# Fourteen of 24 branch gates of a hybrid decoder step as seven pairs of seven block products

## The chip, the cores and the metric

The kernel runs on one NeuronCore of a Trainium2 chip. Five engines work side by side on one on-chip memory (SBUF): PE (TensorE, matrix products into PSUM), DVE (VectorE), ACT (ScalarE), POOL (GpSimd) and SP (SyncE, which here issues every DMA, in one queue and in order). The metric is the device time of one execution in microseconds (us), as the median of several runs.

## The reference: what is computed

One layer of a decoder for a prompt of 1024 tokens and a sample group of 8 x 4 tokens, 1056 columns in all, model width 1024. What concerns the change is the mixer block:

```python
h = _rmsnorm(x, norm_g)
p = h @ w_in
cuts = np.cumsum(IN_WIDTHS)[:-1].tolist()
q, k, v, g, su, sv, xq, gt = jnp.split(p, cuts, axis=-1)
...
g_ret, g_sg, g_x = jnp.split(jax.nn.sigmoid(gt + b_gate), N_BRANCH, axis=-1)
merged = g_ret * (o_ret @ w_br_ret) + g_sg * (o_sg @ w_br_sg) + g_x * (o_x @ w_br_x)
return x + merged @ w_o, S_new, v_rows
```

`gt` holds three gates of 1024 channels each, so 3 x 8 tiles of 128 channels. A feed-forward block follows (2 x 2816 channels up, a causal convolution, a gated gelu, down), and a last norm.

## The kernel before

Activations lie transposed: a tile `[128 x 1056]` holds 128 channels (on partitions) of all columns, and 1024 channels are eight tiles. Every product is made from two rounded parts, high and low, of each operand: high x high, high x low, low x high, three matmuls in place of one. `split` (L285) makes the parts: ACT casts to the high one, then POOL (`ptt`, L114) or DVE (`vtt`, L111) subtracts to get the low one. `hops` are the parts of the eight input tiles without the norm's factor; `scaled` (L348) multiplies a product by that factor per column (`rst`) when it is taken out of PSUM, and the norm's gain sits in the weights.

Weights come from DRAM as slabs of `[128 x 1024]` in the order of the table SLABS (L43 ff.). `w_dma` (L132) loads one into `wr` (two buffers), `w_prep` (L140) makes `wh` on ACT (L150) and `wl` on POOL (three buffers each); a slab's load can start only when the subtraction two slabs back has freed its `wr`.

`fm` (L227) makes one tile of 128 output channels: per 128-channel step k three terms by three column chunks (384, 384, 288), so 72 matmuls of a gate over eight k, 36 of a half-slab product over four, into one of two PSUM buffers `mp`. After each k it calls `hook` (L189), where delayed work (`later`) and generators (`gens`, at `rate` steps a hook) put their instructions: cross-attention `xattn`, or `reload`, which reads a branch's output back from DRAM (`opr<-scr`) and splits it. Each engine executes its instructions in the order in which the program is written.

The stretch that matters, in order: eight gates `gb` (with the last heads of the cross-attention woven into them), gates `gc` 0 and 1 (with the reload of the spatial branch's operands `bops`), eight half-slab products `bs`; then in turn a gate `gc` m+2, half a slab of `bx`, and their sum on POOL; eight gates `ga` (the retention operand is reloaded by `rd`, `rs_`); eight products `br` with the merge; the output product `wo`; the feed-forward block. A gate tile `th` is taken from PSUM by DVE, gets its tanh on ACT and stays in SBUF until `gated` multiplies the branch product into it. `slot` (L90) hands out all such tiles from one pool of 40.

The up-projection of the feed-forward block is written another way already. Two output tiles make a pair. Their two slabs, each cut into two halves of the 1024 input channels, are four blocks a11, a12, a21, a22; the operand is cut by halves of the channels and of the columns (528) into four blocks too. The 2x2 product of such blocks takes seven block products instead of eight, with sums of weight blocks (s1 to s4, `f_sums`, `f_prep0` to `f_prep3`) and of operand blocks (B11, B21, B22, T1 to T4, split by `x_split`). `prod` makes one block product: four k, three terms, two chunks of 264 columns, 24 matmuls into a PSUM buffer `bp`; `put` takes it out on ACT, or on DVE with an addition.

Names in the rows: `ap` is a PSUM buffer of the attention (two of them), `xt`, `xmx`, `xrc`, `pt`, `ox`, `ys` its tiles, `ssq` and `c` tiles of the feed-forward block, `x2c` the residual.

Of the kernel before, what the change touches and what calls it, by code (L numbers as in the profile page):

```python
# [42 lines left out]
def slab_order():  # L43
# [8 lines left out]
    o += [("gc", 0), ("gc", 1)]  # L52
    o += [("bs", j) for j in range(4)]
    for m in range(8):
        if m < 6:
            o += [("gc", m + 2)]
        if m % 2 == 0:
            o += [("bx", m // 2)]
    o += [("ga", m) for m in range(8)]
# [19 lines left out]
def step_kernel(ctx: ExitStack, tc: tile.TileContext, xT, memT, wslab, cst, ident_d, rope, vec, sgc, sgm, sgs,  # L79
# [50 lines left out]
    raws, hil, wst = {}, {}, {"d": 0, "p": 0, "live": 0, "end": FAST0, "max": 3}  # L130
# [41 lines left out]
    gens = deque()  # L172
# [179 lines left out]
    with tc.manual_schedule():  # L352
# [780 lines left out]
        def gate(key, br, m):  # L1133
            ps = fm(key, hops)
            t = slot("th")
            scaled(t, ps)
            act(t, t, AF.Tanh, scale=0.5, bias=vecs[:, VBG + 8 * br + m:VBG + 8 * br + m + 1])
            return t

        def gated(t, ps):  # L1140
            for o, i in zip(seg(t), psv(ps)):
                stt(o, o, 1.0, i, ALU.add, ALU.mult)

        bops, cops, aops = [], [], []
        acc, thc = [], []
        for m in range(8):
            acc.append(gate(("gb", m), 1, m))
        bg = reload([8 + g for g in range(4)], bops)
        cg = reload([12 + g for g in range(4)], cops)
        drain()  # L1150
        rate[0] = 0.5
        gens.append(bg)
        thc.append(gate(("gc", 0), 2, 0))
        thc.append(gate(("gc", 1), 2, 1))
        drain()
        rate[0] = 0.0
        for m in range(8):
            ps = fm(("bs", m // 2), bops, kbase=4 * (m % 2), free=(m % 2 == 1))
            gated(acc[m], ps)
            if m in (1, 3, 5, 7):  # L1160
                next(cg)
        gens.append(cg)
        rate[0] = 1.0
        for m in range(8):
            if m < 6:
                thc.append(gate(("gc", m + 2), 2, m + 2))
            drain()
            ps = fm(("bx", m // 2), cops, kbase=4 * (m % 2), free=(m % 2 == 1))
            gated(thc[m], ps)
            ptt(acc[m], acc[m], thc[m], ALU.add)  # L1170

        raw = {}

# [8 lines left out]
        def late():
            for k in range(2, 8):
                rs_(k)
                rd(k + 3)
                yield

        tha = []
        rate[0] = 1.0
        for m in range(8):  # L1190
            if m == 3:
                rd(0)
                rd(1)
                rd(2)
            if m == 5:
                rs_(0)
                rd(3)
            if m == 6:
                rs_(1)
                rd(4)  # L1200
            if m == 7:
                gens.append(late())
            tha.append(gate(("ga", m), 0, m))
        drain()
        mops = [[], []]
        for m in range(8):
            ps = fm(("br", m), aops)
            gated(tha[m], ps)
            vtt(acc[m], acc[m], tha[m], ALU.add)

            for half in range(2):
                t = slot("mg", F32R)
                src = acc[m][:, half * HW:(half + 1) * HW]
                nc.scalar.copy(out=t[:, 0:HW], in_=src)
                ptt(t[:, HW:2 * HW], src, f(t)[:, 0:HW], ALU.subtract)
                mops[half].append(t)


        x2c = []
        for m in range(8):  # L1220
            x2c.append(slot("x2c"))
            dma(x2c[m], xT[m])
        ssq = slot("ssq")
        hsl = slot("hist")
        dma(hsl[:, 0:NHC], hist)
        hv_ = hsl[:, 0:NUP * 16].rearrange("p (m b j) -> p m b j", b=8, j=2)
        coll = slot("coll", shape=[P, NUP, 18])

        X = {}

        def hs(k, half):
            return x2c[k][:, half * HW:(half + 1) * HW]
# [17 lines left out]
        nrm = {}  # L1250

        def norm_sums(half):
            s3 = nrm["s3"] = slot("ns3", F32R)
            src = ssq[:, half * HW:(half + 1) * HW]
            nc.scalar.copy(out=s3[:, 0:HW], in_=src)
            vtt(s3[:, HW:2 * HW], src, f(s3[:, 0:HW]), ALU.subtract)

        def norm_root(half):
            s3, t = nrm["s3"], slot("nst")
            r = rst[:, half * HW:(half + 1) * HW]  # L1260
            for q in range(2):
                a = ap()[:, 0:QW]
                c = slice(q * QW, (q + 1) * QW)
                mm(a, ones, s3[:, q * QW:(q + 1) * QW], stop=False)
                mm(a, ones, s3[:, HW + q * QW:HW + (q + 1) * QW], start=False)
                rstd_sum(a, r[:, c], t[:, c])
            newton(r, t[:, 0:HW], t[:, HW:2 * HW])

        def h_scale(k, half):
            stt(hs(k, half), hs(k, half), vecs[:, VNF + k:VNF + k + 1], rst[:, half * HW:(half + 1) * HW], ALU.mult, ALU.mult)  # L1270

        def half_norm():

            low = lambda k: x_low(("B11", "B21")[k // 4], k % 4, hs(k, 0), vtt)
            norm_sums(0)
            yield
            norm_root(0)
            for k in range(8):
                h_scale(k, 0)
                x_split(("B11", "B21")[k // 4], k % 4, hs(k, 0), None)  # L1280
                if k:
                    low(k - 1)
                yield
            low(7)

# [44 lines left out]
        def f_prep3(j):  # L1330
# [660 lines left out]
```

## Time and profile before

| What | us |
|---|---|
| median of 3 runs | 1932.78 (1932.71 to 1933.3) |
| profiled execution, its time | 1929.98 |
| profiled execution, its span | 1928.2 |
| granted TensorE clock, mean | 0.994 of full speed |
| PE busy | 1870.1 |
| DVE, POOL, ACT busy | 1055.6, 913.3, 620.0 |

A timeline row gives start, length, engine, line, operation, result tile <- source tiles, size and type, how many (x4), and in brackets how long the engine was idle before and what released it. The rows of section 6 of the page name a DMA, how many, KB each, and the median us from its issue to its landing. The page's slices of the span, 48.2 us each, show where the edit lies, in slices 16 to 24 (690 to 1135 us):

```profile
PE   8999999999999999999999999999999999999997
...
DVE  7464636443464441111112257999999999744447
...
POOL 2343434232643425334264444477777778753404
PEclk9999999999999999999999999999999999999998
...
GB/s 197 44 45 99 37 113 45 113 66 155 56 136 86 110 36 154 34 55 45 89 89 45 182 139 100 34 73 84 78 82 75 77 90 98 260 144 89 76 1 91
```

### The profile page before, as it was taken

The numbers are of one execution on the slowest core, as the hardware profiler recorded it, in microseconds if no ns is written. First come the engines' busy times: TensorE is split into PE (matmuls) and PEld (weight loads), VectorE is DVE, ScalarE is ACT, GpSimd is POOL, SyncE is SP. The second block draws the span as 40 slices with busy tenths as digits, with TensorE's granted clock in tenths as the row PEclk, the third lists the DMA queues.
The fourth block names the chain that finished last, engine by engine and source line by source line (L and its number), as shares of the span: only waits on it lengthen the run. The fifth ranks groups of instructions, "written<-read, shape, count | busy, mean of one in ns | idle before, by whom it ended". The sixth has DMA issues, their size and how long they took to land.

```text
span 1928.2 us, 31394 instructions
## 1 busy us (share of the span) xinstructions
PE 1870.1 (97%) x13201; PEld 1844.8 (96%) x13201; DVE 1055.6 (55%) x1509; ACT 620.0 (32%) x966; POOL 913.3 (47%) x569
## 2 busy tenths in 40 slices
PE   8999999999999999999999999999999999999997
PEld 8999998999999999999999999899999999899996
DVE  7464636443464441111112257999999999744447
ACT  6322232422233432111231234534344344321204
POOL 2343434232643425334264444477777778753404
PEclk9999999999999999999999999999999999999998
DMA  5113131324132314111221443122222223742202
GB/s 197 44 45 99 37 113 45 113 66 155 56 136 86 110 36 154 34 55 45 89 89 45 182 139 100 34 73 84 78 82 75 77 90 98 260 144 89 76 1 91
DMA packets 51741, 174.51 MB, mean 91 GB/s; under 512 B 5712, under 2 KB 8944, under 8 KB 51600
## 3 DMA queue, kind: packets, MB, share of 16 engines
q1 hardware_dynamic: 51600, 172.50, 26.5%
q8 instruction: 104, 1.70, 0.4%
q14 instruction: 37, 0.30, 0.0%
HBM read 137.04 MB, written 35.43 MB: 89 GB/s over the span
## 4 chain that ended last, share of the span: by engine, by line
PE 80%; DVE 11%; ACT 4%; issue 3%; POOL 1%; DMA 0%; DVEq 0%; SPq 0%; ACTq 0%; POOLq 0%
PE mp L106 56%; PE bp L106 20%; PE ap L106 4%; DVE c L118 1%; DVE xl L112 1%; DVE x2c L118 1%; ACT sw L476 1%; ACT wh L150 0%; DVE ssf L112 0%; DVE fs L112 0%; DVE st L526 0%; DVE rt L118 0%; PE ap L576 0%; DVE x L112 0%; DVE th L112 0%
## 5 line engine op out<-in xcount | busy, mean ns | idle before, releaser
L115 POOL TENSOR_TENSOR wl<-wr,wh 128x1024 fp32r<-128x1024 f32 x114 | 297.1, 2610 | 474.8 <-ACT wh L150 410.6
L106 PE MATMUL mp<-hh,wh 128*128 128x384 f32 (+1 forms) x1152 | 261.3, 334 | 5.8 <-ACT hh L109 5.8
L106 PE MATMUL mp<-hl,wh 128*128 128x384 f32 (+1 forms) x1152 | 253.0, 327 | 0.0
L106 PE MATMUL mp<-hh,wl 128*128 128x384 f32 (+1 forms) x1152 | 250.1, 324 | 0.0
L106 PE MATMUL bp<-xh,wh 128*128 128x264 f32 (+2 forms) x1040 | 212.5, 285 | 4.5 <-DVE z L112 2.1
L106 PE MATMUL bp<-xh,wl 128*128 128x264 f32 (+2 forms) x1040 | 212.2, 286 | 0.1
L106 PE MATMUL bp<-xl,wh 128*128 128x264 f32 (+2 forms) x1040 | 211.5, 285 | 0.0
L106 PEld LDWEIGHTS mp<-hh,wh 128*128 128x128 f32 x1152 | 190.9, 190 | 8.1 <-ACT hh L109 5.8
L106 PEld LDWEIGHTS mp<-hh,wl 128*128 128x128 f32 x1152 | 193.4, 189 | 0.0
L106 PEld LDWEIGHTS mp<-hl,wh 128*128 128x128 f32 x1152 | 192.2, 189 | 1.1 <-DVE hl L118 1.1
L112 DVE TENSOR_TENSOR x<-x,mp 128x288 f32<-128x288 f32 (+3 forms) x167 | 105.6, 675 | 120.1 <-PE mp L106 120.1
L106 PEld LDWEIGHTS bp<-xh,wh 128*128 128x128 f32 x1040 | 163.2, 189 | 5.4 <-DVE z L112 2.3
L106 PEld LDWEIGHTS bp<-xh,wl 128*128 128x128 f32 x1040 | 162.8, 189 | 0.3 <-POOL wl L115 0.3
L106 PEld LDWEIGHTS bp<-xl,wh 128*128 128x128 f32 x1040 | 163.0, 189 | 0.0
L115 POOL TENSOR_TENSOR wl<-fs,wh 128x1024 fp32r<-128x1024 f32 x41 | 118.3, 2886 | 47.9 <-ACT wh L1301 47.9
L150 ACT CAST wh<-wr 128x1024 fp32r<-128x1024 f32 x100 | 104.0, 1042 | 76.2 <-PE mp L106 35.9
L106 PE MATMUL mp<-ach,whs 128*128 128x384 f32 (+3 forms) x524 | 123.7, 325 | 4.2 <-DVE x L112 3.4
L118 DVE SCALAR_TENSOR_TENSOR c<-z,hist,c 128x1024 f32<-128x1024 f32 x88 | 123.9, 1408 | 1.6 <-ACT c L109 1.5
L106 PE MATMUL mp<-acl,whs 128*128 128x384 f32 (+3 forms) x524 | 123.2, 325 | 0.0
L106 PE MATMUL mp<-ach,wls 128*128 128x384 f32 (+3 forms) x524 | 123.1, 324 | 0.0
L112 DVE TENSOR_TENSOR th<-mp,rst 128x768 f32<-128x768 f32 (+1 forms) x48 | 31.6, 701 | 164.8 <-PE mp L106 144.2
L118 DVE SCALAR_TENSOR_TENSOR th<-th,mp 128x768 f32<-128x768 f32 (+1 forms) x48 | 31.6, 701 | 145.8 <-PE mp L106 145.8
(355 smaller groups left out, 4066.0 us busy)
## 6 DMA issues: line engine op xcount, KB each, us to landing
wr<-in_wslab SPq DMA_DIRECT2D x162, 512.0 KB, 3.6
sca<-c SPq DMA_DIRECT2D x22, 528.0 KB, 3.0
opr<-sca SPq DMA_DIRECT2D x22, 528.0 KB, 4.5
opr<-scr SPq DMA_DIRECT2D x16, 528.0 KB, 5.0
scr<-ort SPq DMA_DIRECT2D x8, 528.0 KB, 7.6
x2c<-in_xT SPq DMA_DIRECT2D x8, 528.0 KB, 7.4
scx<-x2c SPq DMA_DIRECT2D x16, 264.0 KB, 3.1
x<-scx SPq DMA_DIRECT2D x8, 528.0 KB, 6.7
```

Of the source, the lines that this page charges most:

```text
L106: nc.tensor.matmul(out=out, lhsT=l, rhs=r, start=start, stop=stop)
L112: nc.vector.tensor_tensor(out=out, in0=a, in1=b, op=op)
L115: nc.gpsimd.tensor_tensor(out=out, in0=a, in1=b, op=op)
L118: nc.vector.scalar_tensor_tensor(out=out, in0=a, scalar=s, in1=b, op0=op0, op1=op1)
L150: nc.scalar.copy(out=hi, in_=raw)
L476: nc.scalar.copy(out=o[a:a + 64], in_=i[b:b + 64])
```

## The change

The gates `gc` 2 to 7 and `ga` 0 to 7 become seven pairs, numbered from NG = 100, each made by seven block products with the functions of the up-projection. Those functions (`x_split`, `xop`, `f_dma`, `f_parts`, `f_quads`, `f_sums`, `f_prep0` to `f_prep3`, `prod`, `put`, `blocks`) are the same as before, but move up ahead of the gates; `prod` gets a switch for its chunks.

The block products need operands that are already normalized, since their sums mix the halves of the columns. So the eight input tiles are loaded again (`g_load`, in gb6's hooks), multiplied by gain and column factor (`g_scale`, in gb7's hooks), and the block sums and splits are made in the hooks of gc0 and gc1 and in those of the first pair (`todo`).

All gates now go to DRAM (`sg`) and are read back (`g_get`) behind the pairs, in the loops `bs`, `bx` and `br`, which no longer have gates between them. The branch operands are reloaded later: `bops` in the last pair, `cops` in `bs`, the retention operand in `bx`. The sum in `bx` moves from POOL to DVE. The PSUM pool is closed and opened anew on both sides of the pairs.

```diff
-    o += [("gc", 0), ("gc", 1)]
+    o += [("gc", m) for m in range(8)]
+    o += [("ga", m) for m in range(8)]
     o += [("bs", j) for j in range(4)]
...
+    o += [("bx", j) for j in range(4)]
     o += [("br", m) for m in range(8)]
...
+PAIRS = {j: (("up", j), ("up", NFF + j)) for j in range(1, NFF)}
+NG = 100
+GKEYS = [("gc", m) for m in range(2, 8)] + [("ga", m) for m in range(8)]
+PAIRS.update({NG + i: (GKEYS[2 * i], GKEYS[2 * i + 1]) for i in range(len(GKEYS) // 2)})
...
+        if side:
+            (side.popleft() or int)()
...
+        def gate_out(t, key):
+            br, m = BR[key[0]], key[1]
+            act(t, t, AF.Tanh, scale=0.5, bias=vecs[:, VBG + 8 * br + m:VBG + 8 * br + m + 1])
+            later(3, lambda: dma(sg[br][m], t))
...
+        def g_load():
+            hg.append(slot("hx"))
+            dma(hg[-1], xT[len(hg) - 1])
+        def g_scale(k):
+            stt(hg[k], hg[k], vecs[:, VNM + k:VNM + k + 1], rst, ALU.mult, ALU.mult)
+        gh = lambda k, half: hg[k][:, half * HW:(half + 1) * HW]
+        G0s = lambda k: x_split(("B11", "B21")[k // 4], k % 4, gh(k, 0), vtt)
+        def g1(k):
+            vtt(gh(k, 0), gh(k, 1), gh(k, 0), ALU.subtract)
...
+        for m in range(8):
+            if m == 6:
+                side.extend([g_load] * 8)
+            if m == 7:
+                side.extend([lambda k=k: g_scale(k) for k in range(8)])
+            gate(("gb", m))
+        drain()
+        rate[0] = 0.0
+        side.extend([lambda: f_dma(NG), lambda: G0s(0), lambda: G0s(1), lambda: G0s(2), lambda: (G0s(3), f_prep0(NG)),
+                     lambda: G0s(4), lambda: G0s(5), both(G0s, 6)])
+        gate(("gc", 0))
+        side.extend([lambda: gsum.append(f_sums(NG, vtt, vtt)), lambda: gsum[0](), lambda: f_prep2(NG), both(g1, 0),
+                     both(g1, 2), lambda: f_prep3(NG), both(g2, 0), both(g2, 2)])
+        gate(("gc", 1))
+        pctx.close()
+        bpp = pctx.enter_context(tc.tile_pool(name="bpp", bufs=3, space=bass.MemoryType.PSUM))
+        todo = deque([
+            both(B22s, 0), both(B22s, 2), both(G2s, 0), both(G2s, 2), lambda: f_prep1(NG), both(g3, 0), both(g3, 2), None,
+            both(G3s, 0), both(G3s, 2), None, None, both(g4, 0), both(g4, 2), both(G1s, 0), both(G1s, 2),
+            None, both(G4s, 0), both(G4s, 2)])
...
+        for j in range(NG, NG + len(GKEYS) // 2):
...
+            put(pr("a11", "B11"), p1)
+            if first:
+                ta = slot("th")
+                put(pr("a12", "B21"), lo(ta), p1)
+                put(pr("s4", "B22"), hi_(ta))
+                put(pr("s2", "T2"), r, p1)
+                f_prep0(j + 1)
+            else:
+                put(pr("s2", "T2"), r, p1)
+                if last:
+                    next(bg)
+                ta = slot("th")
+                put(pr("a12", "B21"), lo(ta), p1)
...
+            put(pr("s3", "T3"), u3, r)
...
+            n = pr("s1", "T1")
...
+            put(pr("a22", "T4"), lo(tb), u3)
+            gate_out(tb, kb)
+            fw.pop(j)
+        pctx.close()
+        mpp = pctx.enter_context(tc.tile_pool(name="mpp3", bufs=2, space=bass.MemoryType.PSUM))
...
+        for m in range(8):
+            g_get(acc, 1, m + 3)
+            if m in (1, 3, 5, 6, 7):
+                next(cg, None)
+            if m > 5:
+                g_get(thc, 2, m - 5)
             ps = fm(("bs", m // 2), bops, kbase=4 * (m % 2), free=(m % 2 == 1))
             gated(acc[m], ps)
...
             gated(thc[m], ps)
-            ptt(acc[m], acc[m], thc[m], ALU.add)
+            vtt(acc[m], acc[m], thc[m], ALU.add)
```

Three places show what moves. First DVE in gate gb7, where the attention's last head is woven in (`pt`, `xmx`, `xrc`, `xt`, `ox` are its steps, `th<-mp,rst` the gate before). Before:

```order
L112 TENSOR_TENSOR th<-mp,rst 128x288
L112 TENSOR_TENSOR pt<-ap,pt 128x512
L959 TENSOR_REDUCE xmx<-ap 128x2
L964 RECIPROCAL xrc<-xsm 128x2
L966 TENSOR_SCALAR xt<-xt,xrc 128x256 x2
L1001 COPY ox<-ap 128x256
```

After, the same place:

```order
L114 TENSOR_TENSOR th<-mp,rst 128x288
L120 SCALAR_TENSOR_TENSOR hx<-hx,vecs,rst 128x1056
L114 TENSOR_TENSOR pt<-ap,pt 128x512
L120 SCALAR_TENSOR_TENSOR hx<-hx,vecs,rst 128x1056
L963 TENSOR_REDUCE xmx<-ap 128x2
L120 SCALAR_TENSOR_TENSOR hx<-hx,vecs,rst 128x1056
L968 RECIPROCAL xrc<-xsm 128x2
L970 TENSOR_SCALAR xt<-xt,xrc 128x256 x2
L120 SCALAR_TENSOR_TENSOR hx<-hx,vecs,rst 128x1056
L1005 COPY ox<-ap 128x256
```

A scaling of a whole reloaded tile stands between the steps of the attention.

Second DVE behind gate gc1. Before, the `bs` products follow (their rows are `th<-th,mp`); after, the first pair (`hx` are the normalized tiles and their block sums, `t_` tiles T2, `xl` low parts, rows from `bp` are `put`):

```order
L114 TENSOR_TENSOR th<-mp,rst 128x288
L114 TENSOR_TENSOR xl<-hx,xh 128x528 x4
L114 TENSOR_TENSOR xl<-t_7279,xh 128x528 x2
L114 TENSOR_TENSOR xl<-t_7291,xh 128x528 x2
L114 TENSOR_TENSOR hx<-hx 128x528 x4
L114 TENSOR_TENSOR th<-bp,zt 128x528
L114 TENSOR_TENSOR xl<-hx,xh 128x528 x4
L114 TENSOR_TENSOR hx<-hx,t_7279 128x528 x2
L114 TENSOR_TENSOR hx<-hx,t_7291 128x528 x2
L114 TENSOR_TENSOR xl<-hx,xh 128x528 x4
L114 TENSOR_TENSOR zt<-bp,zt 128x528
L114 TENSOR_TENSOR xl<-hx,xh 128x528 x4
```

Between two operations that read PSUM stand up to twelve that read SBUF alone.

Third SP's queue where the `bx` stage's operands and gates are asked for, before (in gate gc0 and behind it):

```order
L103 DMA opr<-scr_188 128x1056
L103 DMA opr<-scr_189 128x1056
L103 DMA wr<-in_wslab 128x1024
L103 DMA opr<-scr_190 128x1056
L103 DMA wr<-in_wslab 128x1024
L103 DMA opr<-scr_191 128x1056
```

and after (`th<-sg` are gates that come back):

```order
L105 DMA th<-sg_5562 128x1056
L105 DMA opr<-scr_188 128x1056
L105 DMA opr<-scr_189 128x1056
L105 DMA th<-sg_5563 128x1056
L105 DMA wr<-in_wslab 128x1024
L105 DMA th<-sg_5564 128x1056
L105 DMA opr<-scr_190 128x1056
L105 DMA th<-sg_5565 128x1056
L105 DMA wr<-in_wslab 128x1024
```

A gate's load now stands between each two loads of slabs and operands.

More of the change, by code (lines that the diff above doesn't have):

```diff
@@ L1130, in step_kernel @@
             gens.append(xattn(m))
[L1133 to L1161, printed above, removed]
@@ L1182, in late @@
[L1182 to L1219, printed above, removed]
@@ L1248, in xop @@
             return [t[:, (k % 2) * HW:(k % 2 + 1) * HW] for t in X[name][k // 2]]
[L1250 to L1284, printed above, removed]
         fraw, fw = {}, {}
         def f_dma(j):
-            if j < NFF:
+            if j in PAIRS:
                 fraw[j] = [wp.tile([P, 1024], F32, tag="wr", name="wr", bufs=2) for _ in range(2)]
-                for t, key in zip(fraw[j], (("up", j), ("up", NFF + j))):
+                for t, key in zip(fraw[j], PAIRS[j]):
                     dma(t, wslab[SLABS.index(key)])
@@ new lines, in put, with blocks @@
+        def put(ps, out, tmp=None):
+            if tmp is None:
+                nc.scalar.copy(out=quarters(out), in_=ps[:, :, 0:QW])
+            else:
+                vtt(quarters(out), ps[:, :, 0:QW], quarters(tmp), ALU.add)
+        def blocks(j):
+            tp, tu = slot("zt"), slot("zu")
+            return tp[:, 0:HW], tp[:, HW:2 * HW], tu[:, 0:HW], tu[:, HW:2 * HW]
+        bops, cops, aops = [], [], []
+        sg = [[dp.tile([P, T], F32, name=f"sg{b}{m}") for m in range(8)] for b in range(3)]
@@ new lines, in do, with g_get @@
+        def do():
+            for e in wait:
+                e[0] -= 1
+            while wait and wait[0][0] <= 0:
+                wait.pop(0)[1]()
+            if todo:
+                (todo.popleft() or int)()
+        acc, thc, tha = [], [], []
+        bg = reload([8 + g for g in range(4)], bops)
+        cg = reload([12 + g for g in range(4)], cops)
+        def g_get(lst, br, n):
+            while len(lst) < min(n, 8):
+                lst.append(slot("th"))
+                dma(lst[-1], sg[br][len(lst) - 1])
@@ new lines, in step_kernel, with rd, rs_ @@
+        raw = {}
+        def rd(k):
+            if k < 8:
+                raw[k] = slot("opr")
+                dma(raw[k], scr[k])
+        def rs_(k):
+            aops.append(split(raw.pop(k), "op"))
+        for m in range(8):
+            g_get(thc, 2, m + 3)
+            if m == 0:
+                for k in range(3):
+                    rd(k)
+            else:
+                rs_(m - 1)
+                rd(m + 2)
+            if m > 5:
+                g_get(tha, 0, m - 5)
+            ps = fm(("bx", m // 2), cops, kbase=4 * (m % 2), free=(m % 2 == 1))
+            gated(thc[m], ps)
+            vtt(acc[m], acc[m], thc[m], ALU.add)
@@ new lines, in step_kernel @@
+        rs_(7)
+        mops = [[], []]
+        for m in range(8):
+            g_get(tha, 0, m + 3)
+            ps = fm(("br", m), aops)
+            gated(tha[m], ps)
+            vtt(acc[m], acc[m], tha[m], ALU.add)
+            for half in range(2):
+                t = slot("mg", F32R)
+                src = acc[m][:, half * HW:(half + 1) * HW]
+                nc.scalar.copy(out=t[:, 0:HW], in_=src)
+                ptt(t[:, HW:2 * HW], src, f(t)[:, 0:HW], ALU.subtract)
+                mops[half].append(t)
@@ new lines, in step_kernel, with hs, norm_sums @@
+        x2c = []
+        for m in range(8):
+            x2c.append(slot("x2c"))
+            dma(x2c[m], xT[m])
+        ssq = slot("ssq")
+        hsl = slot("hist")
+        dma(hsl[:, 0:NHC], hist)
+        hv_ = hsl[:, 0:NUP * 16].rearrange("p (m b j) -> p m b j", b=8, j=2)
+        coll = slot("coll", shape=[P, NUP, 18])
+        def hs(k, half):
+            return x2c[k][:, half * HW:(half + 1) * HW]
+        nrm = {}
+        def norm_sums(half):
+            s3 = nrm["s3"] = slot("ns3", F32R)
+            src = ssq[:, half * HW:(half + 1) * HW]
+            nc.scalar.copy(out=s3[:, 0:HW], in_=src)
+            vtt(s3[:, HW:2 * HW], src, f(s3[:, 0:HW]), ALU.subtract)
@@ new lines, in norm_root, with h_scale @@
+        def norm_root(half):
+            s3, t = nrm["s3"], slot("nst")
+            r = rst[:, half * HW:(half + 1) * HW]
+            for q in range(2):
+                a = ap()[:, 0:QW]
+                c = slice(q * QW, (q + 1) * QW)
+                mm(a, ones, s3[:, q * QW:(q + 1) * QW], stop=False)
+                mm(a, ones, s3[:, HW + q * QW:HW + (q + 1) * QW], start=False)
+                rstd_sum(a, r[:, c], t[:, c])
+            newton(r, t[:, 0:HW], t[:, HW:2 * HW])
+        def h_scale(k, half):
+            stt(hs(k, half), hs(k, half), vecs[:, VNF + k:VNF + k + 1], rst[:, half * HW:(half + 1) * HW], ALU.mult, ALU.mult)
```

164 lines of the change are left out of this document (107 added, 57 removed).

## Prediction

> **What bounds the kernel now.** I read the page first, then the chain of waits, then the stretch that is edited. From the page, the rows of busy time (engine, us, share, instructions) and of the chain that ended last:
>
> ```profile
> PE 1870.1 (97%) x13201; PEld 1844.8 (96%) x13201; DVE 1055.6 (55%) x1509; ACT 620.0 (32%) x966; POOL 913.3 (47%) x569
> ...
> PE 80%; DVE 11%; ACT 4%; issue 3%; POOL 1%; DMA 0%; DVEq 0%; SPq 0%; ACTq 0%; POOLq 0%
> ```
>
> TensorE is the bound. Where the edit lies, the chain is one unbroken piece of matmuls (start, length, what), and the windows say the same (length, busy time of each engine, clock, DMA share, GB/s; the first is gate gb7 with attention steps between, the second from gate gc1's end to the end of the `br` products, the third the block products of the up-projection):
>
> ```profile
> 715.13 419.31 PE mp L106 x2688
> ...
> 698.70:715.30 16.60, 16.60 (x130) 16.32 (x129) 5.30 (x14) 4.46 (x9) 2.56 (x2) 1.00 0.11 33
> 738.00:1088.00 350.00, 350.00 (x2170) 350.00 (x2169) 59.31 (x84) 67.02 (x71) 140.16 (x65) 1.00 0.20 67
> 1270.00:1630.00 360.00, 360.00 (x2960) 360.00 (x2959) 333.02 (x373) 148.23 (x242) 276.24 (x177) 1.00 0.25 79
> ```
>
> In the second window TensorE never idles, at full clock, while VectorE is busy 17% and GpSimd 40% of it. So each matmul microsecond taken out is a microsecond won, and each new wait is one lost: there is no old wait to hide in. The price of a gate is the distance between VectorE's evacuations (gc0, gc1, then two `bs` half-products):
>
> ```profile
> 726.99 1.32 DVE L112 TENSOR_TENSOR th<-mp,rst 128x768 f32<-128x768 f32 x2 [10.40 <-PE mp L106]
> 738.62 1.32 DVE L112 TENSOR_TENSOR th<-mp,rst 128x768 f32<-128x768 f32 x2 [10.30 <-PE mp L106]
> 744.44 1.32 DVE L118 SCALAR_TENSOR_TENSOR th<-th,mp 128x768 f32<-128x768 f32 x2 [4.50 <-PE mp L106]
> 750.26 1.32 DVE L118 SCALAR_TENSOR_TENSOR th<-th,mp 128x768 f32<-128x768 f32 x2 [4.50 <-PE mp L106]
> ```
>
> 72 matmuls take 11.63 us, 36 take 5.82: 161.6 ns each. The price of a pair by seven products stands in the up-projection, which works this way already: one evacuation comes once a pair, right as its product ends.
>
> ```profile
> 1281.92 0.71 DVE L112 TENSOR_TENSOR z<-bp,zu 128x528 f32<-128x528 f32 x1 [0.54 <-PE bp L106]
> 1302.37 0.71 DVE L112 TENSOR_TENSOR z<-bp,zu 128x528 f32<-128x528 f32 x1 [0.26 <-PE bp L106]
> 1322.81 0.71 DVE L112 TENSOR_TENSOR z<-bp,zu 128x528 f32<-128x528 f32 x1 [0.64 <-PE bp L106]
> ```
>
> 168 matmuls in 20.44 us, 121.7 ns each, 2.92 us a product.
>
> **The gain.** Fourteen gates: 14 x 11.64 = 162.9 us go. Seven pairs: 7 x 20.44 = 143.1 us come. **-19.8 us.** No other product changes.
>
> The Trainium skill, "TensorE: Matmul & The Clock Gate", section "Back-to-back issue gap", gives N/2.4 + 2.5 ns for an isolated matmul; by that estimate a pair of gates would be 21.5 us, a pair of block products 18.9, and the gain 18.1 us instead of 19.8. The rows are longer on both sides (23.3 and 20.44 us), and I use them.
>
> **What is added, step by step.**
>
> *gb7: eight scalings.* VectorE now multiplies eight reloaded 128x1056 inputs, one per hook of gb7, placed between the attention steps. No row shows this; a pair of evacuations over 1056 columns is 1.32 us, so 1.3 us each, 10 us in all, into a window where VectorE was busy 5.30 of 16.60. As work it fits; the cost is order. These are the attention's rows there (GpSimd, VectorE, TensorE):
>
> ```profile
> 702.27 2.40 POOL L115 TENSOR_TENSOR wl<-wr,wh 128x1024 fp32r<-128x1024 f32 x1 [3.40 <-PE ap L106]
> ...
> 703.32 0.68 DVE L959 TENSOR_REDUCE xmx<-ap 128x2 f32<-128x512 f32 x1
> 705.09 0.17 DVE L964 RECIPROCAL xrc<-xsm 128x2 f32<-128x2 f32 x1 [1.09 <-ACT xt L109]
> 705.29 0.62 DVE L966 TENSOR_SCALAR xt<-xt,xrc 128x256 f32<-128x256 f32 x2
> 707.01 0.42 DVE L1001 COPY ox<-ap 128x256 f32<-128x256 f32 x1 [1.11 <-PE ap L106]
> ...
> 708.27 0.60 PE L987 MATMUL ap<-ident,xt 128*128 128x128 f32 x4
> ```
>
> The transposes need the scaled `xt` and the PSUM buffer that the copy `ox` empties. Now one scaling stands ahead of `xmx` (and is held by the `wl` subtraction until 704.67, by the next rows' rule), one behind it, one between `xt` and `ox`. Counted through: `xmx` ends at 706.6, the reciprocal at 708.5, `xt` at 709.1, the scaling at about 710.0, `ox` at 710.4. TensorE wants 708.27 and gets 710.4: **2.1 us**; 1.1 if GpSimd doesn't hold the scaling; nothing if gb7's own matmuls slip in instead, but their order is fixed. I take 2.1.
>
> *How GpSimd and VectorE hinder each other.* The page's ends and the timelines of the up-projection's first pair:
>
> ```profile
> 1218.04 5.03 POOL L115 TENSOR_TENSOR wl<-wr,wh 128x1024 fp32r<-128x1024 f32 x1 [12.89 <-ACT wh L1301]
> ...
> 1217.01 2.56 DVE L112 TENSOR_TENSOR x2c<-x2c,t 128x528 f32<-128x528 f32 x4
> 1219.48 1.32 DVE L112 TENSOR_TENSOR xl<-x2c,xh 128x528 fp32r<-128x528 f32 x2
> 1220.72 0.70 DVE L112 TENSOR_TENSOR z<-bp,zt 128x528 f32<-128x528 f32 x1
> 1221.34 7.25 DVE L112 TENSOR_TENSOR xl<-x2c,xh 128x528 fp32r<-128x528 f32 x9
> ```
>
> A GpSimd subtraction of 2.4 us needs 5.03: it waits 2.6 us through VectorE's back-to-back operations on SBUF, gets in when VectorE reads PSUM (1220.72), and then VectorE's next operations wait until it ends (nine at 0.62 are 5.6, and took 7.25). I take this as the rule for the first pair: GpSimd starts when VectorE idles or reads PSUM.
>
> *Start of the pairs.* The old PSUM pool closes, so the first product waits for gc1's evacuation. The same change of pool stands ahead of the up-projection, with a 0.71 us operation:
>
> ```profile
> 1187.04 0.71 DVE L118 SCALAR_TENSOR_TENSOR x2c<-mp,x2c 128x528 f32<-128x528 f32 x1 [3.72 <-PE mp L106]
> ...
> 1187.90 0.48 PE L106 MATMUL bp<-xh,wh 128*128 128x264 f32 x2 [0.89 <-DVE x2c L118]
> ```
>
> 0.89 us for 0.71; with 1.32 it is **1.5 us**.
>
> *First pair.* Its operands are made while it runs. ScalarE's pace and VectorE's:
>
> ```profile
> 1210.31 2.49 ACT L1239 CAST xh<-t 128x528 fp32r<-128x528 f32 x4 [3.37 <-DVE t L112]
> ...
> 1216.42 0.59 ACT L1413 COPY zt<-bp 128x528 f32<-128x528 f32 x1
> 1216.91 1.05 ACT L1301 CAST wh<-wr 128x1024 fp32r<-128x1024 f32 x1
> ...
> 700.08 1.18 ACT L109 ACTIVATE th<-th,vecs 128x1056 f32<-128x1056 f32 x1 [3.90 <-DVE th L112]
> ```
>
> Casts and VectorE operations on 528 columns are 0.62 each. From the end of gc1's matmuls (time 0): products run 1.5-4.4, 4.4-7.3, 7.3-10.3. ScalarE: tanh to 2.6, B22 casts to 5.1, T2 casts to 7.6, an evacuation to 8.2, the cast of s2, s3 to 9.25. VectorE: B22 and T2 low parts to 8.3, four differences to 10.8, then the first PSUM evacuation. GpSimd's subtraction for s2, s3 is ready at 9.25, starts at 10.8, ends at 13.2; the fourth product wants it at 10.76: **2.5 us**. Meanwhile VectorE waits until 13.2, then does twelve operations to 20.7, evacuates, and here GpSimd's next subtraction gets in (20.7-23.1), so that the T4 low parts begin 2.4 us late and the seventh product loses **2.0 us**. The sums for pair two follow, s2 at 28.1, its subtraction at about 32.2, wanted at 29.9: **2.3 us**. Start and first pair: 1.5 + 2.5 + 2.0 + 2.3 = 8.3 us. Bounds: 1.5 alone where GpSimd always gets in, and 12.6 where pair two repeats the last two.
>
> *Pairs two to seven.* A pair gives VectorE two sums and six PSUM additions (8 x 0.7 = 5.6 us), GpSimd three subtractions of 2.4 and three of half the size (10.8), ScalarE three casts of 1.05, one of 0.62, one evacuation and two tanh (6.7), of 20.44 each. That is less than in the third window above, where the up-projection runs dense with VectorE at 333 and GpSimd at 276 of 360. So these pairs cost nothing beyond their matmuls. Without that cover: one `wl` late, 2.4 us a pair.
>
> *Pairs to `bs`.* The pool changes again, one 0.71 us put: **0.9 us**. The four `bs` operands are loaded in the last pair and land about 9 us into it; four low parts and two slabs on GpSimd, 14.7 us, end at 23.7, or at 26.3 with one more wait of 2.6, and the last of them is wanted at about 26.1. I take nothing, and keep 2.4 us, one such operation, as its bound.
>
> *Reloads.* From the page and the windows:
>
> ```profile
> wr<-in_wslab SPq DMA_DIRECT2D x162, 512.0 KB, 3.6
> ...
> opr<-scr SPq DMA_DIRECT2D x16, 528.0 KB, 5.0
> ...
> 1652.00:1660.00 8.00, 8.00 (x52) 8.00 (x51) 6.00 (x9) 1.65 (x6) 2.41 (x1) 1.00 0.99 372
> ```
>
> The gates now go out (0.54 MB each, one per gate) and come back. In `bs` and `bx`, 16 half-products or 93.1 us, there are 16 gates, 12 operands and 10 slabs to load: 20.4 MB, 219 GB/s, where 372 is shown. Three gates are asked for ahead, 17 us against 5.0 to landing. Hidden behind TensorE. The add of `bx` moves from GpSimd to VectorE: 1.3 us more beside 1.32 in each 5.82. Nothing, in either direction, since neither engine bounds there.
>
> **Sum.** -19.8 + 2.1 + 8.3 + 0.9 = **-8.5 us**. The profiled execution took 1929.98 us (span 1928.2), the median of the three runs is 1932.78, 2.8 above it. So 1921.5 for such an execution and **1924.3 us** for the median.
>
> **Rivals.**
>
> *GpSimd gets in after one VectorE operation.* For it:
>
> ```profile
> 1284.14 2.47 POOL L115 TENSOR_TENSOR wl<-fs,wh 128x1024 fp32r<-128x1024 f32 x1 [2.38 <-ACT wh L1301]
> ...
> 1284.27 2.40 DVE L118 SCALAR_TENSOR_TENSOR c<-zs,hist,c 128x32 f32<-128x32 f32 x1
> ```
>
> Here it waited for 0.1 us between two VectorE operations; against it the 5.03 above. Then s2, s3 are ready at 12.1, 1.3 late, the later ones 1.8 together, gb7 1.1: 1.1 + 1.5 + 1.3 + 1.8 + 0.9 = 6.6, so -13.2, **1919.6 us**. With no stall but the two pool changes, -17.4 and 1915.4, its lower end. The Trainium skill, "SBUF — State Buffer", section "Who interferes with whom", has it so: the shared port is a lock held for a whole instruction, and issue order decides who blocks. The blocked rows agree with the lock; the 5.03 us row, in which VectorE started several operations before it, does not agree with the order.
>
> *The preparation stays behind.* If pair two repeats the late sums (4.3), gb7 loses 4 and the `bs` operands 2.4, the stalls are 11.3 + 4.3 + 1.9 + 2.4 = 19.9: **1932.9 us**, no change; half of it gives 1928.6.
>
> *Slower: the one queue.* All loads and stores are issued in order by SyncE, and a slab's load waits for GpSimd's `wl`. Gate reloads now stand behind such waits. If `bs` and `bx` are fed at 180 GB/s, they last 113 us, 20 more: **1944 us**. It decides from 201 GB/s downward (101.6 us, the whole gain), slower by over 0.2% below 193. For it: the wait row of SyncE on `wl`,
>
> ```profile
> SPq L103 <- POOL wl L115: 449.1, 45, 17.1
> ```
>
> up to 17.1 us long; against it 372 GB/s and the lead of three gates.
>
> *It does not do what it says:* if 264 columns cost what the wide chunks cost, 168 x 161.6 ns = 27.1 us a pair, +27 us. Against it the 20.44 us rows; I fold it into the slower case.
>
> **Numbers.** Forecast (1921 to 1928) 0.60; GpSimd let in (1915.4 to 1921) 0.20; no change 0.13; slower 0.07. What a measurement of this kernel can tell is about 0.2%, 3.9 us: faster 0.80, same 0.13, slower 0.07. Range 1916.0 to 1930.5: it takes in the bounds of the first pair and half of the third case.
>
> **What would show it.** Evacuations of a pair 20.4 us apart from pair two on (wrong: over 21); TensorE waiting on GpSimd's `wl` once in the fourth product and on `xl` in the seventh of the first pair; transposes of gb7 waiting for `ox`; `bs` and `bx` at 5.82 us a product and idle TensorE there under 2 us. A wait of TensorE on a DMA in `bs` would make the slower case true.

## The result and the profile after

| | before | changed |
|---|---|---|
| median, us | 1933.04 (1932.71 to 1936.15, 4 runs) | 1923.43 (1923.15 to 1924.92, 4 runs) |
| profiled execution, its time, us | 1929.98 | 1923.41 |
| its span, us | 1928.2 | 1921.5 |

The ratio is 0.9948 (95% interval 0.9931 to 0.9965): 0.5% faster. The forecast was 1924.3. The two profiled executions differ by 6.6 us, the medians by 9.6: before's profiled execution is one of its shorter ones; over all comparisons its executions reach from 1928.64 to 1936.15 (the last section says what moves them). The ledger below is made between the two profiled executions. One of the four executions of experiment 6's kernel took 5120.84 us, and the record doesn't show why; its ratio rests on the other three.

From the page of the changed kernel, busy time of the engines, then the chain that ended last:

```profile
PE 1855.3 (97%) x13369; PEld 1827.1 (95%) x13369; DVE 1165.2 (61%) x1606; ACT 653.5 (34%) x1016; POOL 935.5 (49%) x587
...
PE 50%; DVE 7%; issue 1%; POOL 1%; ACT 1%; DMA 0%; DVEq 0%; POOLq 0%; ACTq 0%
```

TensorE is busy 14.8 us less, VectorE 110 us more. Before, one unbroken piece of matmuls covered 715 to 1134. The chain of the changed kernel, in order of time (start, length, what), has a piece of VectorE and GpSimd work in its place:

```profile
746.46 1.32 DVE xl L114 x2
...
750.88 4.07 DVE xl L114 x4
...
755.48 4.15 DVE hx L114 x3
...
769.56 2.85 POOL wl L117
...
772.46 115.90 PE bp L108 x954
...
888.37 2.40 POOL wl L117
890.77 2.41 POOL opl L117
...
898.01 228.34 PE mp L108 x1506
```

So the first pair (739 to 767) and the second product of pair two are set by the engines that make its operands, from 772.46 on TensorE is dense for 115.9 us, and at 888 to 898 the operands of `bs` are only just in time. TensorE's waits from 690 to 1130, by who ended them (us in total, times, longest):

```profile
PE bp L108 <- DVE xl L114: 2.4, 2, 1.9
PE bp L108 <- POOL wl L117: 2.1, 2, 1.6
PE bp L108 <- DVE th L114: 1.9, 1, 1.9
PE ap L108 <- ACT xt L111: 1.3, 1, 1.3
PE mp L108 <- DVE th L114: 0.9, 1, 0.9
PE mp L108 <- POOL opl L117: 0.5, 1, 0.5
...
```

No DMA is among them directly. The waits in their places, on TensorE's timeline (the bracket is the idle time and what ended it):

```profile
738.53 0.65 PE L108 MATMUL mp<-hh,wl 128*128 128x384 f32 x3
741.07 0.48 PE L108 MATMUL bp<-xh,wh 128*128 128x264 f32 x2 [1.89 <-DVE th L114]
...
752.57 0.51 PE L108 MATMUL bp<-xh,wl 128*128 128x264 f32 x2 [0.49 <-POOL wl L117]
...
760.30 0.51 PE L108 MATMUL bp<-xl,wh 128*128 128x264 f32 x2 [1.88 <-DVE xl L114]
...
763.26 0.51 PE L108 MATMUL bp<-xl,wh 128*128 128x264 f32 x2 [0.50 <-DVE xl L114]
...
772.46 0.52 PE L108 MATMUL bp<-xh,wl 128*128 128x264 f32 x2 [1.60 <-POOL wl L117]
...
892.40 0.72 PE L108 MATMUL mp<-oph,wh 128*128 128x384 f32 x3 [0.89 <-DVE th L114]
```

From gc1's last matmul (739.18, the end of the first row) to the first `bs` matmul (892.40) are **153.2 us**; this stretch is what the experiments compare. The dense pairs are seen where VectorE adds the second product of pairs four, five and six to its block:

```profile
815.96 0.71 DVE L114 TENSOR_TENSOR zt<-bp,zt 128x528 f32<-128x528 f32 x1 [5.18 <-PE bp L108]
836.31 0.71 DVE L114 TENSOR_TENSOR zt<-bp,zt 128x528 f32<-128x528 f32 x1 [5.16 <-PE bp L108]
856.68 0.71 DVE L114 TENSOR_TENSOR zt<-bp,zt 128x528 f32<-128x528 f32 x1 [5.17 <-PE bp L108]
```

20.36 us a pair, 142.5 for seven, so 10.7 of the 153.2 are lost.

One loss was not in the forecast at all. Two windows of TensorE (length, busy PE, PEld, DVE, ACT, POOL, clock, DMA share, GB/s), the first product and the next two:

```profile
741.07:745.59 4.52, 4.52 (x25) 4.52 (x25) 2.85 (x5) 4.52 (x8) 0.00 (x0) 0.62 0.29 120
745.59:751.50 5.91, 5.91 (x51) 5.91 (x50) 5.91 (x10) 4.86 (x8) 3.39 (x1) 1.00 0.00 1
```

Behind the wait of 1.89 us TensorE's granted clock fell to half for 3.4 us, and the first product took 4.52 us in place of 2.91.

### The profile page after: what moved, and what is told of

The parts are those of the page before. It is cut to its first block, busy times and chain, and to the rows that moved or that the text cites. A ratio compares the mean times of both kernels' runs of the same rounds, so it can differ in the third digit from the quotient of the medians.

```text
span 1921.5 us, 32104 instructions
## 1 busy us (share of the span) xinstructions
PE 1855.3 (97%) x13369; PEld 1827.1 (95%) x13369; DVE 1165.2 (61%) x1606; ACT 653.5 (34%) x1016; POOL 935.5 (49%) x587
## 4 chain that ended last, share of the span: by engine, by line
PE 50%; DVE 7%; issue 1%; POOL 1%; ACT 1%; DMA 0%; DVEq 0%; POOLq 0%; ACTq 0%
PE bp L108 26%; PE mp L108 24%; DVE c L120 1%; DVE xl L114 1%; DVE x2c L120 1%; DVE ssf L114 0%; DVE fs L114 0%; DVE x2c L114 0%; DVE x L114 0%; DVE hx L114 0%; POOL wl L117 0%; DMA wr<-in_wslab 0%; POOL opl L117 0%; POOL acl L117 0%; POOL wls L117 0%
## 5 line engine op out<-in xcount | busy, mean ns | idle before, releaser
L108 PE MATMUL bp<-xh,wh 128*128 128x264 f32 (+1 forms) x1376 | 279.6, 284 | 6.3 <-DVE z L114 2.1
L108 PE MATMUL bp<-xh,wl 128*128 128x264 f32 (+1 forms) x1376 | 281.2, 286 | 2.2 <-POOL wl L117 2.1
L108 PE MATMUL bp<-xl,wh 128*128 128x264 f32 (+1 forms) x1376 | 280.9, 285 | 2.4 <-DVE xl L114 2.4
L108 PE MATMUL mp<-hh,wh 128*128 128x384 f32 (+1 forms) x816 | 189.6, 340 | 5.2 <-ACT hh L111 5.2
L117 POOL TENSOR_TENSOR wl<-fs,wh 128x1024 fp32r<-128x1024 f32 x55 | 155.9, 2836 | 69.4 <-ACT wh L1171 68.9
L108 PE MATMUL mp<-hl,wh 128*128 128x384 f32 (+1 forms) x816 | 179.9, 328 | 0.3 <-DVE hl L120 0.2
L108 PE MATMUL mp<-hh,wl 128*128 128x384 f32 (+1 forms) x816 | 177.7, 325 | 0.0
L108 PEld LDWEIGHTS mp<-hl,wh 128*128 128x128 f32 x816 | 136.8, 190 | 1.4 <-DVE hl L120 1.4
L108 PEld LDWEIGHTS mp<-hh,wl 128*128 128x128 f32 x816 | 137.1, 190 | 0.0
L1171 ACT CAST wh<-fs 128x1024 fp32r<-128x1024 f32 x55 | 57.9, 1053 | 160.4 <-DVE fs L114 149.0
L120 DVE SCALAR_TENSOR_TENSOR c<-zs,hist,c 128x32 f32<-128x32 f32 x88 | 110.8, 1259 | 0.0
```

The source lines that it names most:

```text
L108: nc.tensor.matmul(out=out, lhsT=l, rhs=r, start=start, stop=stop)
L117: nc.gpsimd.tensor_tensor(out=out, in0=a, in1=b, op=op)
L120: nc.vector.scalar_tensor_tensor(out=out, in0=a, scalar=s, in1=b, op0=op0, op1=op1)
L1171: nc.scalar.copy(out=hi, in_=src)
```

## The experiments

Two theories stood against each other. By the theory of **single waits** each wait of TensorE has its own cause and is worth what it lasts. By the theory of **preparation** VectorE and GpSimd, each holding up the other, set when the first pair and the start of pair two can run, and a wait that is taken out there comes back at the next operand. All edits are to the changed kernel. Times of single executions carry clock drops from elsewhere, so the stretch is compared, not the total.

**1. First product in the attention's PSUM buffers.**

```diff
-            put(pr("a11", "B11"), p1)
+            put(prod(fw[j]["a11"], "B11", [ap(), ap()], ...) if first else pr("a11", "B11"), p1)
```

(`prod` and `put` take the two buffers as a list)

> The first block product of the first pair goes into two PSUM buffers of the attention, so that it does not wait for the old PSUM pool to close. In the changed kernel TensorE waited 1.89 us there and then ran its first product in 4.52 instead of 2.91 us at half clock. From gc1's last matmul (739.18) to the first bs matmul (892.40) the changed kernel takes 153.2 us. Theory of single waits: that stretch falls by 3.5 us (1.89 + 1.61), to about 149.7. Theory of preparation (VectorE and GpSimd together, one holding up the other, set when pair two can run, at 772.5): the stretch stays within 1 us of 153.2, since the waits on wl and xl behind it grow by what is taken out here.

TensorE's timeline in this run:

```profile
739.32 0.40 PE L108 MATMUL ap<-xh,wh 128*128 128x264 f32 x2
...
752.44 0.81 PE L108 MATMUL bp<-xh,wl 128*128 128x264 f32 x2 [3.63 <-POOL wl L117]
...
772.30 0.51 PE L108 MATMUL bp<-xh,wl 128*128 128x264 f32 x2 [1.60 <-POOL wl L117]
...
892.25 0.72 PE L108 MATMUL mp<-oph,wh 128*128 128x384 f32 x3 [0.89 <-DVE th L114]
```

The first product starts at once, and the fourth waits 3.63 us for the same subtraction for which it had waited 0.49; the clock drop now follows that wait. From 739.49 to 892.25 are 152.8 us, 0.5 less, as the theory of preparation has it: the start had been a wait in front of a later one.

**2. The split of pair two's a11, a12 two products later.**

```diff
                 put(pr("s2", "T2"), r, p1)
-                f_prep0(j + 1)
...
             put(n, hi_(tb), u3)
+            if first:
+                f_prep0(j + 1)
```

> In the first pair the split of pair two's a11, a12 is written two products later, so that GpSimd's subtraction no longer falls between the sums that T1's low parts need (it held VectorE from 756.1 to 758.4). Theory of single waits: the waits on T1's low parts (1.88 + 0.50 us) go and nothing takes their place: 150.8 us from gc1's last matmul to the first bs matmul. Theory of preparation: those two waits shrink, the wait on s2, s3 of pair two (1.60) or one on a11 grows by as much: 152.5 to 153.5 us.

The waits on T1's low parts go, but now one of 4.46 us on `wl` stands in pair two, with a second clock drop at its end, 6.8 us long (TensorE's timeline):

```profile
770.84 0.81 PE L108 MATMUL bp<-xh,wl 128*128 128x264 f32 x2 [4.46 <-POOL wl L117]
```

From 740.44 to 896.39 are 155.9 us, 2.7 worse. The move itself neither won nor lost: pair two's first product goes on 30.4 us behind gc1's last matmul here (740.44 to 770.84), its second one 33.3 us behind in the changed kernel (739.18 to 772.46), and a product takes 2.9. That is the theory of preparation; the 2.7 arise behind that point, where the clock drop lies. Both theories missed the total: the one said a gain of 2.4, the other no change.

**3. All weights for the first pair, and those made in it, on VectorE.**

```diff
-lambda: f_prep1(NG), both(g3, 0)
+lambda: f_prep1(NG, sub=vtt), both(g3, 0)
...
-                f_prep0(j + 1)
+                f_prep0(j + 1, sub=vtt)
...
-                s34 = f_sums(j + 1, vtt)
+                s34 = f_sums(j + 1, vtt, vtt if first else ptt)
```

(and likewise in gc0, gc1 and for s2, s3 of pair two)

> All weight splits and sums made for the first pair, and those made for pair two during the first pair, go from GpSimd (2.4 us per 128x1024) to VectorE (about 1.25). Theory of single waits: only the two waits on wl go (0.65 and 1.60): 151 us for the stretch from gc1's last matmul to the first bs matmul. Theory of preparation: three subtractions of 2.4 and two of 1.3 become half as long in the first pair, 4.9 us less of the work that bounds it, so 147.5 to 149.5 us, and the waits that are left stand at the pool change and at most one xl. A third way: VectorE becomes late with the PSUM evacuations and the waits move to bp buffers, 153 or more.

741.10 to 892.23, 151.1 us, as the single waits would have it; but the waits are others than that theory leaves. It keeps 1.89, 1.88 and 0.50; there were 1.59 (pool), 1.77 (`xl`), then 0.23 and 0.75 on PSUM buffers that VectorE emptied late and 0.31 on `wl`, and a clock drop followed the 1.77. By the theory of preparation the stretch should have been 147.5 to 149.5. By itself this run decides nothing.

**4. Gap in the scalings of gb7.**

```diff
-                side.extend([lambda k=k: g_scale(k) for k in range(8)])
+                gs = [lambda k=k: g_scale(k) for k in range(8)]
+                side.extend([gs[0], None, None] + gs[1:5] + [both(g_scale, 5)])
...
-        side.extend([lambda: f_dma(NG), lambda: G0s(0),
+        side.extend([lambda: (f_dma(NG), g_scale(7)), lambda: G0s(0),
```

> The second and third scaling are not put ahead of and behind the maximum of the attention's softmax in gb7; they follow four hooks later, the last one in gc0. Theory of order (one scaling ahead of the maximum, held by wl, made the exponential late): gb7, from evacuation to evacuation, falls from 18.35 to 16.6 to 17.1 us, and gc0, gc1 stay at 11.7 and 11.6 to 12.0. Rival: VectorE has too much in gb7 whatever the order, so the wait comes back at another attention step or in gc0, and the sum of gb7, gc0 and gc1 (42.1) stays within 0.5 us.

VectorE's evacuations of gb6, gb7, gc0 and gc1 here:

```profile
699.08 1.32 DVE L114 TENSOR_TENSOR th<-mp,rst 128x768 f32<-128x768 f32 x2 [0.16 <-POOL p L117]
716.75 1.31 DVE L114 TENSOR_TENSOR th<-mp,rst 128x768 f32<-128x768 f32 x2
727.31 1.32 DVE L114 TENSOR_TENSOR th<-mp,rst 128x768 f32<-128x768 f32 x2
738.94 1.32 DVE L114 TENSOR_TENSOR th<-mp,rst 128x768 f32<-128x768 f32 x2 [2.82 <-PE mp L108]
```

From gb6's evacuation to gc1's last matmul (738.90) are 39.8 us, 41.65 in the changed kernel, 39.9 before; the wait of 1.3 us on `xt` is gone. gb7 alone reads 17.67, because VectorE took its tile about 1.1 us late, behind the two scalings put together (gc0 reads 10.56 for it); TensorE lost nothing by that. So the order of the scalings cost the time, not their amount. The last scaling in gc0 cost the first pair nothing either: 152.2 us.

**5. No low parts of T1, T3, T4** (leaves out part of the computation, as the expectation says).

```diff
-        G1s = lambda k: x_split("T1", k, gh(k, 0), vtt)
+        G1s = lambda k: x_split("T1", k, gh(k, 0), None, False)
```

(G3s, G4s likewise; `xop` then gives B22's low part)

> Leaves out part of the computation: the low parts of T1, T3 and T4 are not made (B22's stand in for them), 12 of VectorE's operations of 0.62 us in the first pair, 7.4 us; products, casts, sums and weights stay. Theory of preparation: VectorE and GpSimd are up to 7.4 us ahead from T3 on, so the waits on xl (1.88 and 0.50) and on pair two's wl (1.60) go, while the first three (pool 1.89, clock 1.61, wl 0.49) stay: 148 to 149.5 us from gc1's last matmul to the first bs matmul (153.2). Rival (the wait on pair two's wl is GpSimd's own chain of cast and subtraction): only the waits on xl go, 150.5 to 151.

All of TensorE's waits on the products of this run, with the start of `bs`:

```profile
741.59 0.48 PE L108 MATMUL bp<-xh,wh 128*128 128x264 f32 x2 [1.90 <-DVE th L114]
...
753.10 0.51 PE L108 MATMUL bp<-xh,wl 128*128 128x264 f32 x2 [0.47 <-POOL wl L117]
...
887.60 0.71 PE L108 MATMUL mp<-oph,wh 128*128 128x384 f32 x3 [0.89 <-DVE th L114]
```

From 739.69 to 887.60 are 147.9 us, 0.1 below what the theory of preparation gave. Taking work from VectorE alone also removed the wait for GpSimd's `wl` in pair two. That is the theory of preparation, and the rival (150.5 to 151) is out.

**6. The same work spread out.** Runs 3 and 4 together; besides, the first pair's weight sums in gc0 and half of the T3 differences in gc1.

```diff
+                     lambda: G0s(4), lambda: G0s(5), lambda: (G0s(6), G0s(7), gsum.append(f_sums(NG, vtt, vtt)))])
...
+        side.extend([lambda: gsum[0](), lambda: f_prep2(NG, sub=vtt), both(g1, 0), both(g1, 2),
+                     lambda: f_prep3(NG, vtt), both(g2, 0), both(g2, 2), both(g3, 0)])
```

> Weight splits on VectorE (as in the run before), scalings with the gap (as in the run before), and besides the weight sums moved from gc1 to gc0 and half of the differences for T3 from the first pair to gc1, so that VectorE has 1.3 us less in the first pair. Theory of preparation: gb6's evacuation to gc1's last matmul 39.9 us (41.65 in the changed kernel), gc1's last matmul to the first bs matmul 145 to 147.5 us (153.2; 151.1 with the weights on VectorE alone), no drop of TensorE's clock in the first pair: 1914 to 1917 us. Rival (the 1.77 us wait on T1's low parts has another cause than VectorE's queue): 150 to 151 us, 1919 to 1921.

1915.48 us, ratio to before 0.9908 (0.9893 to 0.9923): the best version measured. 39.85 us up to gc1's end (697.47 to 737.32), then 149.7 (to 887.04): between the forecasts. The largest wait in the pairs is 1.50, and TensorE's clock doesn't drop there. So preparation sets the stretch, but this theory put the worth of relieving it too high here and in run 3.

**7. And 8. Both ends in the attention's buffers.** Run 7: run 6, with all of the T3 differences in gc1, and the first and the last product as in run 1. Run 8: run 6, with the last product so, and the second `bs` slab split after the last `bs` operand (`w_prep` behind the sixth product).

> As the spread run, with all differences for T3 in gc1, and the first product of the first pair and the last of the last pair in the attention's PSUM buffers. Now that VectorE is ahead, the two waits for a PSUM pool (1.5 to 1.9 and 0.89 us) should be worth what they last, other than in the first run of this kind: 142.5 to 144.5 us from gc1's last matmul to the first bs matmul, 1911 to 1915 us. Rival (preparation still sets the first pair): the waits move to xl or wl again and the stretch stays where the spread run has it.

> The spread run, with the last product of the last pair in the attention's PSUM buffers and the second bs slab split after the last bs operand. The wait for the PSUM pool before bs (0.89 us) goes, and the wait on opl (0.32) doesn't grow, since GpSimd's operand comes 2.4 us earlier: 1.0 to 1.2 us less than the spread run, 1914.4 us. Rival: opl takes the place of the pool, as it did in the run with both (1.47 us): no change against the spread run, 1915.5.

1915.95 us (ratio 0.9916, 0.9903 to 0.9930) and 1916.95 (0.9922, 0.9906 to 0.9937): no gain on run 6 by either. The stretch fell by 1.0 us in each, to 148.8 and 148.7 (run 7 was to reach 142.5 to 144.5), and what was won there was lost again behind it. In run 7 the start wait gave way to waits of 1.01 and 0.51 for the fourth product's weights, with a clock drop behind them, and the pool wait before `bs` to one of 1.47 on `opl`:

```profile
747.52 0.51 PE L108 MATMUL bp<-xh,wh 128*128 128x264 f32 x2 [1.01 <-ACT wh L1171]
...
892.94 0.75 PE L108 MATMUL mp<-opl,wh 128*128 128x384 f32 x3 [1.47 <-POOL opl L117]
```

In run 8 a wait of 0.68 on `wl` and one of 1.38 on a PSUM buffer took the place of 0.89 and 0.32, not `opl`, as its rival had said:

```profile
900.77 0.73 PE L108 MATMUL mp<-oph,wh 128*128 128x384 f32 x3 [1.38 <-DVE th L120]
```

At this end GpSimd's queue is one bound (in the changed kernel seven subtractions of 2.4 in a row, 883.5 to 900.3). The 1.38 comes from a landing: VectorE empties that buffer at 899.30, behind the first gate that comes back, which was asked for at 893.55 and landed at 899.17; its request had stood behind a slab load that waited for GpSimd's subtraction.

**9. And 10. Twice the reloads.** The slower rival turned on whether `bs` and `bx` can be fed. First each gate was read back twice into the same tile:

```diff
                 dma(lst[-1], sg[br][len(lst) - 1])
+                dma(lst[-1], sg[br][len(lst) - 1])
```

> Each gate is read back from DRAM twice, into the same tile: 0.54 MB more for each of 24 loads, so 16 x 0.54 = 8.7 MB more in bs and bx, 29 MB in 93 us, 312 GB/s where 372 was shown. If the reloads have the room that the forecast gave them, bs and bx stay at 5.8 us a product and the time within 2 us of the changed kernel. If the one queue is near its limit, TensorE waits on DMA or on GpSimd's low parts of late operands there, and the 93 us grow by 5 or more.

1949.27 us, and 234 GB/s in 892 to 985. SyncE's waits from 890 to 1010 tell why:

```profile
SPq L105 <- DMA th<-sg: 81.5, 15, 7.8
...
```

Each second read waited at the head of the queue until the first had landed. So the copy was given a tile of its own:

```diff
+                dma(slot("tx"), sg[br][len(lst) - 1])
```

> In the run before, each second read of a gate went into the same tile, so SyncE waited for the first to land (81.5 us of waits in 890 to 1010) and the run can't tell bandwidth from that wait. Here the second copy goes into a tile of its own that nobody reads: the same 29 MB, 312 GB/s, for bs and bx, without that wait. If the transfers have room (windows of bs in the changed kernel show 374 and 410 GB/s), bs and bx stay at 5.8 us a product and TensorE waits under 2 us there. If 230 GB/s is what this stage can get, the 93 us grow by 20 or more.

The window of `bs` and `bx` then, and the same window in the changed kernel:

```profile
892.00:985.00 93.00, 92.72 (x575) 92.45 (x574) 39.13 (x37) 21.46 (x21) 57.52 (x23) 1.00 0.91 352
```

```profile
892.00:985.00 93.00, 92.10 (x568) 91.85 (x569) 39.17 (x38) 21.54 (x21) 57.41 (x23) 1.00 0.66 249
```

The stage moved 352 GB/s in place of 249, and TensorE was as busy as before. It has room for the transfers; what it has no room for is a landing that the queue waits for.

## Why the prediction was right, step by step

| Step | forecast, us | measured, us |
|---|---|---|
| matmuls of 14 gates, by 7 pairs | -19.8 | -20.4 (162.9 to 142.5) |
| gb7 | 2.1 | 1.7 (18.35 against 16.61) |
| start of the pairs | 1.5 | 1.89, and 1.61 by the clock |
| fourth product, on `wl` | 2.5 | 0.49 |
| sixth, on T1's low parts | 0 | 1.88 + 0.50 |
| seventh, on T4's low parts | 2.0 | 0 |
| pair two, on s2, s3 | 2.3 | 1.60 |
| pairs to `bs` | 0.9 | 0.89 |
| rest of the 10.7 (TensorE's restart behind six waits) | not counted | 1.9 |
| `bs`, `bx`, `br` | 0 | 1.1 (187.3 against 186.2) |

**The gain** came as worked out: a pair takes 20.36 us, where 20.44 was taken from the up-projection.

**The losses** sum to 13.6 where 11.3 was forecast. Their mechanism was right, and run 5 shows it; the terms of the first pair were mis-sized. *Start*: the forecast took 1.5 from the other change of pool; gc1's evacuation itself was 0.4 late behind VectorE's sums (so it is in run 5), and the clock drop was not in the sum. In run 4, where the evacuation is on time, the start wait is 1.51 and the fourth product's 2.01, near the forecast of 1.5 and 2.5. *Fourth product*: GpSimd's subtraction waited behind VectorE's four operations, got in at the PSUM read of 750.17 (worked out from its normal 2.4) and ended at 752.52, 13.3 us behind gc1's last matmul, where 13.2 was forecast; but the product came there 2 us later than forecast, since the start had taken that time. These two terms are one sum, 4.0 forecast, 4.0 measured. *Sixth and seventh*: "GpSimd starts when VectorE idles or reads PSUM" failed here. VectorE's and GpSimd's rows:

```profile
747.70 2.56 DVE L114 TENSOR_TENSOR hx<-hx 128x528 f32<-128x528 f32 x4
750.17 0.71 DVE L114 TENSOR_TENSOR th<-bp,zt 128x528 f32<-128x528 f32 x1
...
754.87 4.77 DVE L114 TENSOR_TENSOR hx<-hx,t 128x528 f32<-128x528 f32 x4
```

```profile
748.11 4.41 POOL L117 TENSOR_TENSOR wl<-fs,wh 128x1024 fp32r<-128x1024 f32 x1 [10.84 <-ACT wh L1171]
755.52 2.94 POOL L117 TENSOR_TENSOR wl<-wr,wh 128x1024 fp32r<-128x1024 f32 x1 [3.00 <-ACT wh L1171]
```

Ready at 748.11, GpSimd waited 2.0 us through three boundaries between VectorE's operations; ready at 755.52, it waited 0.6 and got in amid four operations of the same kind (4.77 us for 2.48). So the held work was T1's, one product earlier than forecast; 2.4 us were lost in place of 2.0 (the 0.50 of them behind a second GpSimd operation, the sum for pair two at 760.95). The Trainium skill, "SBUF — State Buffer", section "Who interferes with whom", says that issue order decides. The second row fits it, the first does not, and why one got in and the other did not stays open. *gb7*: the size was right (1.7 of 2.1), the place was not: TensorE waited not for `ox` but, earlier, for the exponential `xt`, which the held scaling ahead of `xmx` had made late:

```profile
702.19 2.46 DVE L120 SCALAR_TENSOR_TENSOR hx<-hx,vecs,rst 128x1056 f32<-128x1056 f32 x1
704.57 0.68 DVE L963 TENSOR_REDUCE xmx<-ap 128x2 f32<-128x512 f32 x1
```

```profile
706.37 0.50 PE L108 MATMUL ap<-pt,mmh 128*128 128x256 f32 x2 [1.31 <-ACT xt L111]
```

Run 4 shows that the place of the scalings did it.

**Costs taken at nothing.** Pairs two to seven are dense, as forecast, but for the second product of pair two. `bs` lost 1.1 us, of it 0.51 on `opl`, inside the bound of 2.4 that was kept. The DMA rival is refuted by run 10, with 1.4 times as much moved in the same 93 us. But the first landing comes late: VectorE waits for it before it can empty the first `bs` product.

```profile
901.63 1.32 DVE L120 SCALAR_TENSOR_TENSOR th<-th,mp 128x768 f32<-128x768 f32 x2 [9.38 <-DMA th<-sg]
```

That PSUM buffer is free at 902.95, and TensorE wants it at 905.1, when its second product ends: 2 us of reserve, which run 8 used up.

**What evened out.** The losses were 2.3 larger than forecast, the gain 0.6 larger. Besides, the changed kernel was 1.1 us ahead at gb6's evacuation (697.53 against 698.67): in gb3 VectorE made a low part of an attention operand 2.2 us earlier, and TensorE's wait of 1.7 on `xql` is gone (before, ScalarE's cast `xqh` ahead of it waited 2.2 us for GpSimd's `kcl`; in the changed kernel it doesn't). No term of the forecast was for that. A half-clock period at 1161.7, which before's execution doesn't have, took 1.2 us back. -20.4 + 13.6 - 1.1 + 1.2 is -6.7, and the spans differ by 6.7. The median fell by 9.6 since before's profiled execution was shorter than its median, and the changed kernel's was not. By the profiled executions the forecast was 1.9 us too low (1921.5 against 1923.41); that 1923.43 lies within 0.9 of 1924.3 is in part luck.

## What to carry to other kernels

When products are made cheaper by operands that must be prepared first, price the preparation as one chain over the engines that hold each other up, and place it under plain products: here a wait removed at the front came back at the next operand, while moving VectorE's work ahead and taking GpSimd's over took another 5.3 us out of the same two stretches (1.8 of it by the order in gb7, and about 1.6 by the clock drop that no longer comes). Put added work of an engine behind the steps that a latency-bound chain on it is waiting for, not between them. In a queue that issues in order, room in bandwidth says little; look for a landing that its head must wait for.

## What was not expected of the hardware

TensorE's clock drops in windows on a fixed grid. In all twelve profiled executions the half-clock periods begin on a grid of 3.41 us, to within 2 ns, and last one step of it or, four times, two (the last one apart, in which the program ends). Where TensorE stood idle over 1.91 us within one such window, the next one ran at half clock, every time; of the windows with 1.50 to 1.91 us idle some were followed by one and some not, and with less than 1.50 none (counted up to 1880 us, without windows that were at half clock themselves). The wait of 1.88 us at 760.30 straddled two windows, 0.48 and 1.41, and cost nothing more; the wait of 1.89 at 741.07 lay in one and cost 1.61. The Trainium skill, "TensorE: Matmul & The Clock Gate", section "What's actually happening", has the free-running window of this length, but puts the drop after an idle window; here little more than half of one was enough. The grid doesn't start with the program (the first half-clock period begins at 48.26 us in run 10 and at 50.04 in run 8, which is not a whole step apart), so nearly the same wait can cost 1.6 us more in one execution and nothing more in another. In a stage that the edits left alone, from 1155 to 1186 us, seven of the twelve executions have a half-clock period and five, before's among them, have none. This is the likeliest reason for the 7 us between before's own executions. They have no trace, but the record has the mean granted clock of 21 of them: 0.995 in the two shortest of these (1928.6 and 1928.7), 0.991 in the five longest (1935.1 to 1936.0). By an estimate from these figures, 0.004 of 1930 us is 7.7 us.
